# A decoder layer's channel mixer: first product by seven block products for eight, part of the weight sums by accumulating DMA, second product by quarters

## The chip, the cores and the metric

One core of a Trainium2 chip runs the kernel. The metric is device time in microseconds (us) of one execution; the number compared is the median of the runs shown. Engines: PE is TensorE (matmul; PEld is its weight load), DVE is VectorE, ACT is ScalarE, POOL is GpSimd, SP is SyncE, which only issues DMAs here.

## The reference

One inference step of a one-layer decoder: 560 tokens (16 meta, 512 prompt, 32 decode), 1024 channels, 4096 channels in the mixer, all float32. Only the last lines concern the change:

```
h = rms_norm(x, g_mix); proj = h @ w_in            # conv branch and delta-rule branch from proj
...
x = x + mix @ w_o
hm = rms_norm(x, g_mlp) @ w_up                     # first product, 1024 -> 4096
x = x + jnp.square(jax.nn.relu(hm)) @ w_down       # second product, 4096 -> 1024
y = rms_norm(x, g_final)
```

## The kernel before

Channels lie on partitions and tokens on columns. Every large product goes by output tiles of 128 channels by 544 tokens (16 meta tokens are dropped by then), in two halves of 272 tokens (`NPH`). The operands are float32 split in a high and a low part, so each tile of 128 channels of the sum takes three matmuls per half: high weights by high input, high by low, low by high. A tile of a product over 1024 channels is thus 8 x 3 x 2 = 48 matmuls of 128 x 128 weights by 272 columns. They accumulate in a tile `pg` of PSUM with 2 x 512 columns, a half of the tokens in each 512; two such tiles take turns (`psg`, `bufs=2`).

The order of all instructions is written out by a planner at build time (class `Weaver`): streams of work (generators) yield an engine, a modelled cost and what they wait for; the stream whose next instruction could start earliest in the model emits it, and at equal starts the one with the lower priority number. The engines run their queues in that order; semaphores between engines are put in by the framework from the tiles that each instruction reads and writes.

The streams that matter here:

- `weights_dma` (L510) loads one chunk of weights, 128 x 1024, by SP into `wraw`; two chunks are in flight.
- `weights_prep` splits a chunk: ACT writes the high part `wh` (L526), DVE the low part `wl` (L541). For chunks 12 to 61, in earlier stages, ACT writes the negative high part (L535) and POOL adds the chunk to it by an accumulating DMA (L537).
- `gemm` issues the matmuls (L574), and a stream empties each tile of PSUM.
- `ev_wo` (output projection, 8 tiles): DVE adds the tile to the residual `x1` (L1702), ACT and DVE split x1 * g_mlp into `hx` in buffer `R1` (L1706, L1708), ACT squares and DVE sums for the norm (L1715, L1718). `mlp_norm` makes 1 / (mean square + eps) in `r2` (L1728, L1730): it is applied after the second product.
- `ev_up` (first product, 32 tiles): ACT relu from PSUM (L1749), square (L1752), high part (L1754); DVE low part (L1756).
- `ev_dn` (second product): DVE multiplies the tile by `r2` (L1771) and adds it to `x1` (L1774).
- `last_half`: the last tile of the second product goes by halves of the tokens: 48 x 2 matmuls for the first half are followed by those of the second, while DVE empties the first half of the same `pg` tile (L1823), and the final norm of that half begins.

The order of the stages: w_in's products, then w_cout's and w_dout's, then 8 tiles of w_o, 16 tiles of the first product, 8 tiles of the second over the first 2048 channels (two chunks, 96 matmuls each), 16 more of the first, 8 more of the second, and the final norm.

Of the kernel before, what the change touches and what calls it, by code (L numbers as in the profile page):

```python
# [14 lines left out]
P = 128  # L15
# [8 lines left out]
# the first token that the queries need, for their short convolution  # L24
# [8 lines left out]
# columns of the packed per-channel vectors  # L33
# [9 lines left out]
# columns of the packed constants  # L43
# [3 lines left out]
def gemm_order():  # L47
    glu = [[("gb", r), ("ga", r)] for r in range(8)]
    qvz = [[("q", h), ("v", h)] + ([("z", h - 1)] if h else []) for h in range(H)]
    gd = [("gd", c) for c in range(8)]  # L50
    seq = [("k", h) for h in range(8)]
    for x in glu[:6] + qvz[:1] + glu[6:7] + qvz[1:3] + glu[7:] + qvz[3:]:
        seq += x
    seq += gd[:4] + [("z", 7)] + gd[4:]
    for kind in ("do", "gc", "co"):
        seq += [(kind, c) for c in range(8)]
    seq += [("wo", c) for c in range(8)]
    seq += [("up", f) for f in range(16)]
    seq += [("dn0", c) for c in range(8)]
    seq += [("up", f) for f in range(16, 32)]  # L60
    seq += [("dn1", c) for c in range(8)]
    return seq


def n_chunks(kind):
    return 2 if kind in ("dn0", "dn1") else 1


class Tm(float):
    """A modelled time, with the engine that produces it."""  # L70
# [4 lines left out]
class Weaver:  # L75
    """Interleaves in-order streams of instructions by a rough model of the engines."""
# [4 lines left out]
    # how long an engine may wait for a more urgent stream  # L81
# [72 lines left out]
def build(tc, i, o):  # L154
# [15 lines left out]
    with ExitStack() as ctx:  # L170
# [27 lines left out]
        # ---------------------------------------------------------------- constants  # L198
# [13 lines left out]
        # statistics of the delta rule, [token, head, tile]  # L212
# [26 lines left out]
        # ---------------------------------------------------------------- start: x, RMSNorm, h  # L239
# [18 lines left out]
        def warm(n):  # L258
            """Products of ones while the operands come: the tensor engine's clock falls when it rests."""
# [6 lines left out]
        def start():  # L266
# [38 lines left out]
            # sum of squares over channels  # L305
# [52 lines left out]
        def split_x(g, tx, tw):  # L358
            """The parts of x * g_mix, for the first products, whose results take the norm's factor per token."""
# [93 lines left out]
        def mean_bcast(acc, n, rb, ta):  # L453
            """The mean over the channels of acc's sums, on all partitions."""
# [14 lines left out]
        def norm_bcast(acc, rb, t):  # L469
            """1 / sqrt(mean + eps) of acc's sums over the channels, on all partitions."""  # L470
# [26 lines left out]
        # ---------------------------------------------------------------- weights and products  # L497
        seq = gemm_order()
        NW = sum(n_chunks(s[0]) for s in seq)

        def weights_dma():
            yield wait("w_go")
            for n in range(1, NW):
# [7 lines left out]
                E(("raw", n)).set(dma_t(t, 128 * 4096))  # L511

        def weights_prep():
            for n in range(NW):
# [28 lines left out]
                E(("prepl", n)).set(t)  # L543

        rhs_of = {}

        def gemm():
            src_of = {"do": "o", "co": "c", "wo": "m", "up": "x", "dn0": "f0", "dn1": "f1"}
            n = 0
            for idx, (kind, c) in enumerate(seq):  # L550
# [4 lines left out]
                nchk = n_chunks(kind)  # L555
# [3 lines left out]
                steps = [(ch, part, k) for ch in range(nchk) for part in (0, 1) for k in range(8)]  # L559
                # the last product goes by halves of the tokens  # L560
                last = idx == len(seq) - 1
                for h0, h1 in ((0, 1), (1, 2)) if last else ((0, 2),):
                    for ch, part, k in steps:
                        m, row = n + ch, 8 * ch + k
                        if part:
                            tp = yield wait(("prepl", m))
                        else:
                            tp = yield wait(("preph", m) if m else ("preph", 0, k // 4))
                        tk = yield wait((src, row))
                        hi, lo = rhs_of[src](row)  # L570
                        for w, x in ((wls, hi),) if part else ((whs, hi), (whs, lo)):
                            t = yield op("pe", (h1 - h0) * (N / 2400 + 0.0027), tp, tk, tf)
                            for hf in range(h0, h1):
                                nc.tensor.matmul(pt[:, hf, 0:N], w[m][:, k, :], x[:, off + hf * N:off + hf * N + N],  # L574
                                                 start=row == 0 and not part and x is hi,
                                                 stop=row == 8 * nchk - 1 and part == 1)
                        if k == 7:
                            E(("mm" if part else "mmh", m)).set(t)
                    if last:
                        W.spawn(last_half(h0, pt, t), -3 * h0)  # L580
                n += nchk
                if last:
                    W.spawn(warm(NTAIL), -4)
                else:
                    W.spawn(evac(idx, kind, c, pt, t), -3)

        def evac(idx, kind, c, pt, t):
            t = yield from {"k": ev_k, "q": ev_q, "v": ev_v, "z": ev_z, "gb": ev_gb, "ga": ev_ga,
                            "gd": ev_gate, "gc": ev_gate, "do": ev_do, "co": ev_co, "wo": ev_wo, "up": ev_up,
                            "dn0": ev_dn, "dn1": ev_dn}[kind](idx, kind, c, pt, t)  # L590
# [7 lines left out]
        # ---------------------------------------------------------------- beta, g and the decays  # L598
        def g_stage(bk, t):
# [21 lines left out]
            # log(1 + e) = ln(w) + (e - (w - 1)) / w with w = fl(1 + e)  # L621
# [17 lines left out]
            # cumulative sums  # L639
# [28 lines left out]
            # decay matrices of the short segments, all heads: D4[j, h, i]  # L668
# [42 lines left out]
        def d_stage():  # L711
            """Decay matrices D[j, i] = exp(sum of g over (j, i]), zero for i < j."""
# [96 lines left out]
        # ---------------------------------------------------------------- gram matrices of k with their decays  # L809
# [31 lines left out]
        def column_sums(b, sq, sel, t, tb, start=True, stop=True):  # L841
            """Column sums of sq [128, 560] into the rows that sel picks, a quadrant of b for each 128 columns."""
# [23 lines left out]
        def k_norm(hh):  # L866
            """Squared norms of k: columns hh, hh + 8, ... of one bank."""
# [23 lines left out]
        def k_scale(t):  # L891
# [10 lines left out]
            # s = beta / (|k|^2 + 1e-6)  # L902
# [52 lines left out]
        # ---------------------------------------------------------------- (I + K)^-1: blocks of 32 by substitution  # L955
# [105 lines left out]
        # the short segments (decode, prompt tail): blocks of 16 in one lane a head  # L1061
# [922 lines left out]
```

## Time and profile before

| | us |
|---|---|
| median of 3 runs | 1128.67 |
| lowest, highest | 1128.37, 1131.11 |
| span of the profiled execution | 1127.7 |
| output projection, 8 tiles | 677 to 725.5 |
| first product, tiles 0 to 15 | 725.5 to 822.9 |
| second product, first half | 822.9 to 919.4 |
| first product, tiles 16 to 31 | 919.4 to 1016 |
| second product, second half, to its last matmul | 1016 to 1115 |

The span of the profiled execution runs from its first to its last instruction; it is 1.0 us under the median. Idle time of an engine is put down to what ended it.

### The profile page before, as it was taken

The page shows a single profiled execution, that of the slowest core. Times are in us where ns is not written, and L with a number is a line of the kernel's source. Part 1 is how long each engine was busy: PE and PEld are TensorE (multiplying, and loading weights), DVE is VectorE, ACT ScalarE, POOL GpSimd, SP SyncE. Part 2 cuts the span into 40 slices and gives each one's busy share as a digit, 9 for nine tenths or more (in the row PEclk, how much of TensorE's full clock was granted, in tenths as well). Part 3 has the DMA queues.
Part 4 walks back from the last instruction along what each step waited for, and adds up shares of the span by engine and source line. Part 5 has one row for each costly group of instructions (what it writes and reads, how often), then busy time and mean ns, then how long its engine had stood idle before and what let it go on. Part 6 is the DMA issues. An engine that isn't in the chain of part 4 may idle for free.

```text
span 1127.7 us, 21551 instructions
## 1 busy us (share of the span) xinstructions
PE 1097.2 (97%) x8985; PEld 1053.7 (93%) x8985; DVE 663.3 (59%) x1086; ACT 577.1 (51%) x1154; POOL 123.1 (11%) x139
## 2 busy tenths in 40 slices
PE   8999989999989999999899999999999999999996
PEld 6998987999879899999799999999999999999996
DVE  5976996788768877888664355543333233333334
ACT  5586235778768778764247233345421125442320
POOL 2371310102211122221000000000000000000000
PEclk9999998999999999999899999999999999999998
DMA  5223563565556656467624332222332322232222
GB/s 203 76 71 102 123 146 79 126 174 126 143 143 156 149 128 154 135 171 177 151 76 148 100 94 77 92 94 76 94 94 76 94 94 77 93 95 76 94 76 80
DMA packets 49517, 127.71 MB, mean 113 GB/s; under 512 B 13684, under 2 KB 19212, under 8 KB 49420
## 3 DMA queue, kind: packets, MB, share of 16 engines
q1 hardware_dynamic: 42220, 100.12, 28.3%
q0 software_dynamic: 7200, 26.22, 12.5%
q8 instruction: 70, 1.15, 0.4%
q14 instruction: 27, 0.22, 0.1%
HBM read 91.10 MB, written 9.01 MB: 89 GB/s over the span
## 4 chain that ended last, share of the span: by engine, by line
PE 82%; DVE 9%; DMA 5%; issue 2%; ACT 1%; SPq 0%; POOLq 0%; POOL 0%; DVEq 0%; ACTq 0%
PE pg L574 72%; DMA wl<-wraw 2%; DMA wraw<-in_w_dram 2%; DMA M<-in_sd_dram 1%; DMA out_osd_dram<-M 1%; DVE V L1148 1%; DVE M L993 1%; DVE M L990 1%; DVE M L984 1%; DVE RT L997 1%; DVE M L940 1%; PE bk L846 1%; PE bk L1450 1%; PE bk L1370 1%; DVE M L1002 1%
## 5 line engine op out<-in xcount | busy, mean ns | idle before, releaser
L574 PE MATMUL pg<-R,wh 128*128 128x272 f32 (+2 forms) x2944 | 421.0, 294 | 1.6 <-DVE R L427 0.9
L574 PEld LDWEIGHTS pg<-R,wh 128*128 128x128 f32 x2944 | 386.6, 189 | 9.0 <-issue 4.1
L526 ACT ACTIVATE wh<-wraw 128x1024 fp32r<-128x1024 f32 (+1 forms) x153 | 161.3, 1054 | 313.3 <-PE pg L574 239.9
L541 DVE TENSOR_TENSOR wl<-wraw,wh 128x1024 fp32r<-128x1024 f32 x102 | 125.4, 1229 | 175.5 <-PE pg L574 132.7
L574 PE MATMUL pg<-R,wl 128*128 128x272 f32 (+2 forms) x1472 | 218.3, 295 | 0.0
L574 PEld LDWEIGHTS pg<-R,wl 128*128 128x128 f32 x1472 | 197.7, 191 | 3.6 <-issue 2.0
L1148 DVE SCALAR_TENSOR_TENSOR V<-V,vec,V 128x512 f32<-128x512 f32 x240 | 176.1, 767 | 2.9 <-ACT V L1140 0.5
L574 PE MATMUL pg<-RD,wh 128*128 128x272 f32 x512 | 107.9, 291 | 0.5 <-DVE V L1823 0.5
L574 PE MATMUL pg<-K,wh 128*128 128x272 f32 x512 | 108.0, 291 | 0.2 <-DVE K L1678 0.2
L574 PE MATMUL pg<-M,wh 128*128 128x272 f32 x768 | 101.1, 288 | 0.0
L574 PEld LDWEIGHTS pg<-M,wh 128*128 128x128 f32 x768 | 98.2, 188 | 0.0
L574 PEld LDWEIGHTS pg<-RD,wh 128*128 128x128 f32 x512 | 82.1, 191 | 0.8 <-DVE V L1823 0.8
L574 PEld LDWEIGHTS pg<-K,wh 128*128 128x128 f32 x512 | 81.8, 191 | 0.5 <-DVE K L1678 0.5
L537 POOL DMA_DIRECT2D wl<-wraw x50 | 43.7, 874 | 341.7 <-ACT wl L535 199.2
L574 PE MATMUL pg<-RD,wl 128*128 128x272 f32 x512 | 71.7, 292 | 2.2 <-DMA wl<-wraw 2.1
L574 PEld LDWEIGHTS pg<-RD,wl 128*128 128x128 f32 x512 | 67.4, 191 | 2.9 <-DMA wl<-wraw 2.9
L1837 POOL TENSOR_TENSOR ncol<-ncol,misc 68x4 f32<-68x4 f32 x2 | 2.0, 1004 | 536.8 <-DVE ncol L1835 536.8
L535 ACT ACTIVATE wl<-wraw 128x1024 fp32r<-128x1024 f32 x50 | 52.8, 1056 | 4.5 <-PE pg L574 4.5
L1771 DVE TENSOR_TENSOR V<-pg,pre 128x544 f32<-128x544 f32 x15 | 10.9, 725 | 71.4 <-PE pg L574 71.4
L574 PE MATMUL pg<-M,wl 128*128 128x272 f32 x384 | 52.3, 288 | 0.0
L574 PEld LDWEIGHTS pg<-M,wl 128*128 128x128 f32 x384 | 49.9, 188 | 0.0
L783 DVE SCALAR_TENSOR_TENSOR of<-pre,vec,of 128x584 f32<-128x584 f32 x33 | 30.3, 917 | 18.0 <-ACT of L780 17.5
(368 smaller groups left out, 1271.7 us busy)
## 6 DMA issues: line engine op xcount, KB each, us to landing
wraw<-in_w_dram SPq DMA_DIRECT2D x151, 512.0 KB, 3.6
wl<-wraw POOLq DMA_DIRECT2D x50, 512.0 KB, 4.7
M<-in_sd_dram SPq DMA_DIRECT2D x8, 512.0 KB, 4.9
out_osd_dram<-M SPq DMA_DIRECT2D x8, 512.0 KB, 2.8
M<-in_xT_dram SPq DMA_DIRECT2D x8, 280.0 KB, 5.7
V<-in_xT_dram SPq DMA_DIRECT2D x8, 272.0 KB, 5.0
out_oy_dram<-R SPq DMA_DIRECT2D x6, 272.0 KB, 2.3
Ex<-in_sc_dram SPq DMA_DIRECT2D x8, 136.0 KB, 3.8
```

Source lines behind the costliest of these rows:

```text
L526: nc.scalar.activation(wh[:, c[0]:c[1]], w[:, c[0]:c[1]], AF.Copy)
L535: nc.scalar.activation(wl, w, AF.Copy, scale=-1.0)
L537: nc.gpsimd.dma_start(wl, w.bitcast(F32R), accum_op=ALU.add)
L541: nc.vector.tensor_tensor(wl, w, wh.bitcast(F32), op=ALU.subtract)
L574: nc.tensor.matmul(pt[:, hf, 0:N], w[m][:, k, :], x[:, off + hf * N:off + hf * N + N], start=row == 0 and not part and x is hi, stop=row = ...
L783: nc.vector.scalar_tensor_tensor(acc[:, 0:584], pr[:, q:q + 584], vcol(w + q), acc[:, 0:584], op0=ALU.mult, op1=ALU.add)
L846: nc.tensor.matmul(b[32 * j:32 * j + 32, 0:w], sel, sq[:, 128 * j:128 * j + w], start=start, stop=stop)
L940: nc.vector.scalar_tensor_tensor(M1["KT"][:, n, :], b[:, 128 * j:128 * j + 128], st["s"][:, hh, j:j + 1], Ds[hh][:, j, :], op0=ALU.mult, o ...
L984: nc.vector.transpose(L[s].rearrange("p a b -> p a b"), KT[s, :, 32 * q:32 * q + 32].rearrange("p n c -> p c n"))
L990: nc.vector.tensor_tensor(tv, L[:, j + 1:, j:j + 1].to_broadcast([P, n, j + 1]), Tl[:, j:j + 1, 0:j + 1].to_broadcast([P, n, j + 1]), op=A ...
L993: nc.vector.tensor_tensor(Tl[:, j + 1:, 0:j + 1], Tl[:, j + 1:, 0:j + 1], tv, op=ALU.subtract)
L1148: nc.vector.scalar_tensor_tensor(cc[:, 0:512], G[r][:, 16 + q:528 + q], vcol(w + q), cc[:, 0:512], op0=ALU.mult, op1=ALU.add)
```

## The change

The first product goes by groups of two output tiles (`g`, 16 groups). In a group the weights are a 2 x 2 matrix of blocks (output tile by even or odd channel tiles of the input; 4 x 128 channels by 128) and the input another (even or odd channel tiles by halves of the tokens). The 2 x 2 block product is made of seven block products instead of eight, each 4 x 3 = 12 matmuls of 272 columns, by sums of blocks on both sides and of the results:

- Input sums T1 to T4 are made once, by DVE, while the output projection runs (`mix_in`, in place of L1706 and L1708), and split in high and low parts by ACT and DVE.
- Weight sums: `P3` and `P1` come from a load and an accumulating DMA that POOL issues from DRAM onto it (`mlp_sums`); `P2` and `P4` are two more adds on DVE. The seven blocks of a group are split by half-chunks of 512 columns (ACT high, DVE low) into a ring of six.
- The results lie in four accumulators: W and Y are the halves of one `pg` tile, X and Z those of the other. Product 1 goes to X; ACT copies X (`s1`); product 6 is added onto X; ACT copies X (`u2`); product 7 is added; ACT copies X negated (`u3`). W takes product 2, Y product 4, Z product 5. DVE forms the four blocks of the result: C11 from W and `s1`, C21 from Y and `u3`, C22 from Z and `u3`; then product 3 is added onto Z, and DVE forms C12 from Z and `u2`. ACT's relu, square and high part and DVE's low part follow as before, for two tiles a group.
- The order of a group is 1, then 3 of the group before, then 2, 6, 4, 7, 5; in the last group of a set 1, 3 of the group before, 2, 6, 5, 7, 4, 3.
- The second product goes by quarters of its 4096 channels (48 matmuls a tile, 32 tiles in all, each emptied by L1771 and L1774), and the stages are now five groups, quarter 0, four groups, quarter 1, four groups, quarter 2, three groups, quarter 3.
- Buffers are placed anew; comments are taken out. The products up to w_o are unchanged.

The diff, cut to its core:

```
+MLP = [("up", (0, 1, 2, 3, 4)), ("dn", 0), ("up", (5, 6, 7, 8)), ("dn", 1), ("up", (9, 10, 11, 12)), ("dn", 2),
+       ("up", (13, 14, 15)), ("dn", 3)]
+PROD = {1: ("A11", "B11", "X"), 2: ("A12", "B21", "W"), 3: ("P4", "B22", "Z"), 4: ("A22", "T4", "Y"),
+        5: ("P1", "T1", "Z"), 6: ("P2", "T2", "X"), 7: ("P3", "T3", "X")}
+def up_order(groups):
+    out, prev = [], None
+    for g in groups:
+        last = g == groups[-1]
+        out.append((g, 1))
+        if prev is not None:
+            out.append((prev, 3))
+        out += [(g, m) for m in ((2, 6, 5, 7, 4, 3) if last else (2, 6, 4, 7, 5))]
+        prev = g
+    return out
...
+        def mix_in(c, t):
+            t = yield op("act", act_c(NPOST) + 0.07, t)
+            nc.scalar.activation(b[:], x1[c][:], AF.Copy, scale=vcol(V_GMLP + c))
+            t1 = yield op("act", act_c(n), t)
+            nc.scalar.activation(hi, bb, AF.Copy)
...
+            t1 = yield op("dve", dve_c(n), t1)
+            nc.vector.tensor_tensor(lo, bb, hi.bitcast(F32), op=ALU.subtract)
+            if not odd:
+                return
...
+            nc.vector.scalar_tensor_tensor(tb[:, one], ta[:, one], -1.0, b[:, two], op0=ALU.mult, op1=ALU.subtract)
+            nc.vector.tensor_tensor(tb[:, two], tb[:, one], b[:, one], op=ALU.add)
+            nc.vector.tensor_tensor(ta[:, two], b[:, two], b1[:, two], op=ALU.subtract)
+            for q, x, tx in ((6, tb, t), (4, ta, t3)):
+                nc.scalar.activation(a[q], x[:], AF.Copy)
+                nc.vector.tensor_tensor(a[q + 1], x[:], a[q].bitcast(F32), op=ALU.subtract)
...
+        def mlp_sums(g, rb, t):
+            t = yield op("pool", 1.0, t)
+            nc.gpsimd.dma_start(rb, i["wu"][g][:, 1024:2048], accum_op=ALU.add)
...
+                    if nm == "P2":
+                        nc.vector.tensor_tensor(rc[:, 0:512], rb[:, 512:1024], ra[:, 512:1024], op=ALU.add)
+                        nc.vector.tensor_tensor(rc[:, 512:1024], rc[:, 0:512], ra[:, 0:512], op=ALU.add)
...
+                if s >= 6:
+                    tf = yield wait(("bmm", s - 6))
+                nc.scalar.activation(hi, raw, AF.Copy)
+                nc.vector.tensor_tensor(lo, raw, hi.bitcast(F32), op=ALU.subtract)
...
+        def up_gemm(groups):
+            n0, wy, tf0 = yield from pg_tile()
+            n1, xz, tf1 = yield from pg_tile()
+            acc = {"W": (wy, 0), "Y": (wy, 1), "X": (xz, 0), "Z": (xz, 1)}
+            for g, m in up_order(groups):
+                wn, bn, an = PROD[m]
+                pt, hf = acc[an]
+                if m in (6, 7):
+                    tf = yield wait(("upc", g, {6: "s1", 7: "u2"}[m]))
+                elif m == 3:
+                    tf = yield wait(("upc", g, "C22"))
+                elif g != groups[0]:
+                    tf = yield wait(("upc", g - 1, {1: "u3", 2: "C11", 4: "C21", 5: "C12"}[m]))
+                for part in (0, 1):
+                    for kp in range(4):
...
+                        for w, x in ((wl, hi),) if part else ((wh, hi), (wh, lo)):
+                            t = yield op("pe", NPH / 2400 + 0.0027, tp, tk, tf)
+                            nc.tensor.matmul(pt[:, hf, 0:NPH], w[:, kp, :], x,
+                                             start=kp == 0 and not part and x is hi and m not in (3, 6, 7),
+                                             stop=kp == 3 and part == 1, skip_group_check=True)
...
+        def up_copies(g, acc):
+            x = acc["X"][0][:, acc["X"][1], 0:NPH]
+            for k, (nm, m, sc) in enumerate((("s1", 1, 1.0), ("u2", 6, 1.0), ("u3", 7, -1.0))):
+                nc.scalar.activation(up["k"][k][:], x, AF.Copy, scale=sc)
+        def up_c(g, acc, an, nm, m, k, need, dst):
+            a = acc[an][0][:, acc[an][1], 0:NPH]
+            in0, in1, o_ = (up["k"][k][:], a, ALU.subtract) if nm == "C22" else (a, up["k"][k][:], ALU.add)
+            nc.vector.tensor_tensor(dst, in0, in1, op=o_)
...
+        def dn_gemm(q):
+            for c in range(8):
+                n, pt, tf = yield from pg_tile()
+                steps = [(p_, k) for ks in ((0, 1, 2, 3, 4, 5), (6, 7)) for p_ in (0, 1) for k in ks]
```

## Rows read from the trace of the kernel before

**Rows 1.** The page: busy time, share of the span and instructions of each engine; then the chain that ended last, its shares of the span by engine.
```profile
PE 1097.2 (97%) x8985; PEld 1053.7 (93%) x8985; DVE 663.3 (59%) x1086; ACT 577.1 (51%) x1154; POOL 123.1 (11%) x139
PE 82%; DVE 9%; DMA 5%; issue 2%; ACT 1%; SPq 0%; POOLq 0%; POOL 0%; DVEq 0%; ACTq 0%
```
**Rows 2.** Busy time by stretch: length, then PE, PEld, DVE, ACT and POOL busy in us (instructions), granted clock, busy share of the DMA engines, GB/s. An earlier stretch with accumulating DMAs, then the four mixer stages.
```profile
200.00:300.00 100.00, 99.84 (x813) 92.95 (x811) 81.26 (x155) 77.57 (x205) 15.87 (x23) 1.00 0.59 144
...
725.50:822.90 97.40, 97.40 (x773) 96.92 (x772) 36.20 (x36) 48.12 (x65) 0.00 (x0) 1.00 0.28 87
822.90:919.40 96.50, 96.50 (x770) 96.50 (x769) 29.20 (x31) 18.92 (x19) 0.00 (x0) 1.00 0.29 88
919.40:1016.00 96.60, 96.60 (x772) 96.60 (x771) 31.75 (x33) 46.14 (x61) 0.00 (x0) 1.00 0.28 88
1016.00:1100.00 84.00, 84.00 (x671) 84.00 (x670) 29.10 (x32) 25.26 (x29) 0.00 (x0) 1.00 0.26 82
```
**Rows 3.** Timeline of PE in the first product, one tile and the start of the next: start, length, engine, line, operation, number.
```profile
738.68 4.18 PE L574 MATMUL pg<-R,wh 128*128 128x272 f32 x32
742.70 2.17 PE L574 MATMUL pg<-R,wl 128*128 128x272 f32 x16
744.71 4.18 PE L574 MATMUL pg<-R,wh 128*128 128x272 f32 x32
```
**Rows 4.** Timeline of PE, PEld and DVE where the last tile of the second product goes from the first half of the tokens to the second; in brackets the idle time before and what ended it.
```profile
1106.90 0.29 PE L574 MATMUL pg<-RD,wh 128*128 128x272 f32 x1
...
1107.02 0.28 PE L574 MATMUL pg<-K,wh 128*128 128x272 f32 x1
1107.34 0.44 DVE L1823 TENSOR_TENSOR V<-pg,pre 128x272 f32<-128x272 f32 x1 [2.81 <-PE pg L574]
...
1107.84 0.19 PEld L574 LDWEIGHTS pg<-RD,wh 128*128 128x128 f32 x1 [0.75 <-DVE V L1823]
1107.84 0.39 PE L574 MATMUL pg<-RD,wh 128*128 128x272 f32 x1 [0.53 <-DVE V L1823]
...
1108.07 0.29 PE L574 MATMUL pg<-K,wh 128*128 128x272 f32 x1
```
**Rows 5.** Groups of instructions by line from 740 us to the end: number, busy us, mean ns of one, idle before.
```profile
L541 DVE TENSOR_TENSOR wl<-wraw,wh 128x1024 fp32r<-128x1024 f32 x61 | 74.6, 1223 | 147.4 <-PE pg L574 113.5 <-ACT wh L526 23.1 <-issue 10.8
L526 ACT ACTIVATE wh<-wraw 128x1024 fp32r<-128x1024 f32 x60 | 63.7, 1061 | 176.9 <-PE pg L574 176.6
L1749 ACT ACTIVATE zs<-pg 128x544 f32<-128x544 f32 x30 | 18.8, 626 | 28.4 <-PE pg L574 28.4
L1771 DVE TENSOR_TENSOR V<-pg,pre 128x544 f32<-128x544 f32 x15 | 10.9, 725 | 71.4 <-PE pg L574 71.4
L1752 ACT ACTIVATE of<-zs 128x544 f32<-128x544 f32 x15 | 9.9, 659 | 0.5
L1756 DVE TENSOR_TENSOR K<-acc,RD 128x544 fp32r<-128x544 f32 x8 | 5.8, 726 | 6.1 <-ACT RD L1754 6.1
L1827 ACT ACTIVATE zs<-V 128x272 f32<-128x272 f32 x2 | 0.9, 432 | 11.5 <-DVE V L1825 11.5
```
**Rows 6.** DMA issues: number, KB each, median us from issue to landing.
```profile
wraw<-in_w_dram SPq DMA_DIRECT2D x151, 512.0 KB, 3.6
wl<-wraw POOLq DMA_DIRECT2D x50, 512.0 KB, 4.7
```
**Rows 7.** Timeline of all engines where the output projection ends and the first product begins.
```profile
725.53 4.19 PE L574 MATMUL pg<-R,wh 128*128 128x272 f32 x32
725.73 0.73 DVE L1702 TENSOR_TENSOR V<-pg,V 128x544 f32<-128x544 f32 x1 [2.86 <-PE pg L574]
...
726.49 0.76 ACT L1706 ACTIVATE R<-V,vec 128x544 fp32r<-128x544 f32 x1 [1.67 <-DVE V L1702]
727.15 0.64 ACT L1715 ACTIVATE zs<-V 128x544 f32<-128x544 f32 x1
```
**Rows 8.** Timeline of the end on DVE: the last half of the last tile is emptied, and the last eight outputs.
```profile
1115.35 0.44 DVE L1823 TENSOR_TENSOR V<-pg,pre 128x272 f32<-128x272 f32 x1
...
1121.07 2.52 DVE L1851 TENSOR_TENSOR R<-V,bk 128x272 f32<-128x272 f32 x7 [3.15 <-PE bk L1841]
```
**Rows 9.** Timeline of PE after a wait of 2.12 us, in an earlier stage.
```profile
537.95 3.40 PE L574 MATMUL pg<-RD,wl 128*128 128x272 f32 x16 [2.12 <-DMA wl<-wraw]
541.15 0.66 PE L574 MATMUL pg<-RD,wh 128*128 128x272 f32 x2
...
542.05 0.44 PE L574 MATMUL pg<-RD,wh 128*128 128x272 f32 x2
542.34 0.42 PE L574 MATMUL pg<-K,wh 128*128 128x272 f32 x2
```
**Rows 10.** Timeline of PE at a wait of 1.53 us, in the stage of the heads.
```profile
394.04 0.65 PE L1474 MATMUL bk<-M,kq 128*32 128x128 f32 x16 [1.53 <-DMA M<-in_sd_dram]
```
**Rows 11.** Busy time of stretches around these two waits, columns as in Rows 2; the granted clock is the third number from the end.
```profile
540.00:543.00 3.00, 3.00 (x18) 3.00 (x18) 1.58 (x3) 0.06 (x1) 0.00 (x0) 0.65 0.88 225
543.00:546.00 3.00, 3.00 (x27) 3.00 (x26) 2.86 (x5) 2.09 (x3) 0.75 (x1) 1.00 0.36 143
...
365.00:400.00 35.00, 33.47 (x272) 29.94 (x271) 26.70 (x59) 26.50 (x81) 6.20 (x6) 1.00 0.52 127
400.00:450.00 50.00, 50.00 (x404) 46.04 (x404) 39.74 (x80) 42.48 (x126) 13.88 (x12) 1.00 0.62 151
```

More of the change, by code (lines that the diff above doesn't have):

```diff
@@ L498, in build @@
         seq = gemm_order()
-        NW = sum(n_chunks(s[0]) for s in seq)
+        NW = len(seq)
         def weights_dma():
@@ L558, in gemm @@
                 off = Q0 if kind == "q" else META if kind in ("z", "gd", "gc") else 0
[L559 to L564, printed above, removed]
+                for part in (0, 1):
+                    for k in range(8):
                         if part:
-                            tp = yield wait(("prepl", m))
+                            tp = yield wait(("prepl", idx))
@@ L567, in gemm @@
                         else:
-                            tp = yield wait(("preph", m) if m else ("preph", 0, k // 4))
-                        tk = yield wait((src, row))
-                        hi, lo = rhs_of[src](row)
+                            tp = yield wait(("preph", idx) if idx else ("preph", 0, k // 4))
+                        tk = yield wait((src, k))
+                        hi, lo = rhs_of[src](k)
                         for w, x in ((wls, hi),) if part else ((whs, hi), (whs, lo)):
[L572 to L585, printed above, removed]
+                            t = yield op("pe", 2 * (N / 2400 + 0.0027), tp, tk, tf)
+                            for hf in range(2):
+                                nc.tensor.matmul(pt[:, hf, 0:N], w[idx][:, k, :], x[:, off + hf * N:off + hf * N + N],
+                                                 start=k == 0 and not part and x is hi, stop=k == 7 and part == 1)
@@ new lines, in build, with up_tiles @@
+        up = {}
+        def up_tiles(g):
+            if g == 0:
+                yield wait(("wosq", 7))
+            if g == 1:
+                yield wait(("mixin", 3))
+            if g in (5, 9, 13):
+                for c in (6, 7):
+                    yield wait(("dn", (g - 5) // 4, "add", c))
+            if g >= 2:
+                for f in (2 * g - 4, 2 * g - 3):
+                    yield wait(("upr", f))
+            up[g] = [T(x, [P, NPOST]) for x in (("zs0", "zs1") if g % 2 == 0 else ("V8", "V9"))]
+            E(("uptile", g)).set(0.0)
@@ new lines, in up_out1, with up_out2 @@
+        def up_out1(g, acc):
+            yield wait(("uptile", g))
+            c = up[g][0]
+            yield from up_c(g, acc, "W", "C11", 2, 0, "s1", c[:, one_])
+            t = yield from up_c(g, acc, "Z", "C12", 3, 1, "u2", c[:, two_])
+            yield from up_act(2 * g, c, t)
+        def up_out2(g, acc):
+            yield wait(("uptile", g))
+            c = up[g][1]
+            for nm in (("C21", "C22") if g in four_first else ("C22", "C21")):
+                an, m = ("Y", 4) if nm == "C21" else ("Z", 5)
+                t = yield from up_c(g, acc, an, nm, m, 2, "u3", c[:, one_ if nm == "C21" else two_])
+            E(("upc", g, "C22+")).set(t)
+            yield from up_act(2 * g + 1, c, t)
@@ L1744, in ev_up, with f_tile, up_act @@
+        four_first = [g for kind, a in MLP if kind == "up" for g in a[:-1]]
+        def f_tile(f):
+            j = f % 10
+            if ("f", j) not in fhl:
+                fhl[("f", j)] = (T(f"RD{j}", [P, NPOST], F32R)[:], T(f"K{j}", [P, NPOST], F32R)[:]) if j < 8 else ring["f"][j - 8]
+            fhl[f] = fhl[("f", j)]
+            return fhl[f]
+        def up_act(f, c, t):
+            if f >= 10:
+                yield wait(("dnq", (f - 10) // 8))
             if f >= 2:
-                yield wait(("f%d" % ((f - 2) // 16), (f - 2) % 16))
@@ L1763, in ev_dn @@
+        def ev_dn(idx, q, c, pt, t):
             tr = yield wait("r2")
-            E(("dn0m", c)).set(t)
             if c >= 2:
-                yield wait((kind, "add", c - 2))
-            elif kind == "dn1":
-                yield wait(("dn0", "add", 6 + c))
+                yield wait(("dn", q, "add", c - 2))
+            elif q:
+                yield wait(("dn", q - 1, "add", 6 + c))
+            if c < 2:
+                for f in range(8 * q + 4, 8 * q + 8):
+                    yield wait(("upr", f))
```

313 lines of the change are left out of this document (263 added, 50 removed).

## The prediction

> **What bounds the kernel now.** I read the page's busy shares first: PE is busy in 97% of the span, and the chain that ended last lies on it for 82% [rows 1]. The busy time by stretch says where: in all four mixer stages PE is busy in the whole stretch at a granted clock of 1.00 (the upper level, 2.4 GHz), while DVE and ACT stand at 19 to 50% and the DMA engines at 26 to 29% [rows 2]. The timeline gives the rate. One tile of the first product starts at 738.68, the next at 744.71: 48 matmuls in 6.03 us, 125.6 ns each [rows 3]. Inside the mixer nothing but the number of matmuls, or a new wait on PE, can move the end.
>
> **What the change removes.** First product before: 32 tiles x 48 = 1536 matmuls. After: 16 groups x 7 products x 12 = 1344 of the same shape. 192 fewer x 0.1256 = **24.1 us gained**. The second product keeps its count (16 x 96 = 32 x 48).
>
> **What it adds on PE: waits on a PSUM tile.** X and Z are two halves of one tile, W and Y of the other. Before, a mixer tile is filled whole and then emptied whole, so only one place shows what happens when PE fills one half while another engine reads the other: the last tile. There two matmuls of the second half go through, then PE waits until DVE's read of the first half (L1823) has ended, though its own data have long been there [rows 4]. That DVE started only after those two matmuls says the same from the other side. So in this program readers and writers of a two-half tile are kept in order as for one object. The price: the second matmul starts at 1107.02, the fourth at 1108.07, 1.05 us instead of two pitches (0.25): **0.80 us a wait**, with a DVE read of 0.44 us [rows 4].
>
> The Trainium skill speaks against such a wait: in "PSUM — Partial Sum Buffer", sections "PSUM bank collisions raise a hardware error" and "Summary: rules for kernel authors", accesses to different banks run clean and a reader beside running matmuls should target a different bank. A bank is 2 KiB by that page, so the halves are different banks and the chip needs no wait; the row shows that this program waits nevertheless. By the rule the forecast would be the first rival's time, below.
>
> Now the same place in the new order 1(X), 3 of the group before (Z), 2(W), 6(X), 4(Y), 7(X), 5(Z), next 1(X):
> - `s1` reads X after product 1; PE goes on with product 3 in Z: a wait.
> - `u3` reads X after 7; PE goes on with 5 in Z: a wait.
> - C22 reads Z after 5; PE goes on with the next group's 1 in X: a wait.
> - `u2`, C12, C11 and C21 are followed by a product in the other tile, 1.51 us (12 x 0.1256) that cover a read of 0.4 us: nothing.
>
> The first group of a set has no product 3 behind its 1 (no `s1` wait); the last goes 6, 5, 7, 4, 3 and has waits at `s1` and `u2` alone. Per set of n groups that is 3(n - 1) + 1: sets of 5, 4, 4, 3 make 13 + 10 + 10 + 7 = **40 waits**. Most can't be escaped: were the planner to put the `u3` or C22 read (or the last group's `u2`) later than the next product, the product behind that one needs its value. Only the 12 `s1` waits could go, which leaves 28.
>
> Length: an ACT copy of 272 columns from PSUM has no row. 272 from SBUF took 432 ns (L1827); from PSUM 544 took 626 (L1749) against 659 from SBUF (L1752) [rows 5], so some 0.40 and a wait of 0.76. From below 0.76; from above 0.80 plus half of an ACT instruction that happens to run (0.66 / 2), 1.13. I take 0.80: the planner gives these reads the lowest priority number, and ACT and DVE have room (below). **40 x 0.80 = 32.0 us lost**, between 28 x 0.76 = 21.3 and 40 x 1.13 = 45.2. Behind each such wait stand all of PE's later matmuls; for PE wait the next combines, relu and the splits of weights whose ring slot it frees.
>
> **Stage changes.** A set takes both tiles at once, and product 1 goes into X, in the tile that the stage before filled last. So PE waits until that tile is emptied, where before the other tile was free. Three times it is L1771 with 0.725 [rows 5]: 0.80 + 0.725 - 0.44 = 1.08 each, 3.3 us; up to 5.4 if an add of 0.72 stands ahead on DVE. Once it is L1702 with 0.73 [rows 7]: 1.1. There the input of the last channel tile is late too: before, L1706 ran right behind L1702 [rows 7]. Now, counted from the last w_o matmul: L1702 ends at 1.04; on ACT two half-chunks of weights (half of 1.06 each [rows 5]) and the square (0.64) stand ahead of the scaling copy (0.76 [rows 7]), then the high part 0.66, then DVE's low part 0.73 behind two sums of 0.44: ready at some 4.5. PE reaches that operand, the last quarter of product 2, at 1.2 + 1.5 + 0.75 = 3.5. I take 0.9 (0 if nothing stands ahead, 2.5 if every sum does). Stage changes together **5.3 us**, from 4.3 to 9.
>
> **The end.** The last tile's second half now lasts 24 matmuls (3.0 us) instead of 48, so the two final passes of DVE meet. The second begins its last outputs 5.7 us after L1823 [rows 8], when the first's eight (some 3 us) are nearly done: **0.5 us**, 0 to 1.
>
> **What I cost at nothing, and its cover.** ACT in a group: 7 half-chunks x 0.53 + 3 copies x 0.43 + 6 passes of 544 x 0.66 = 9.0 us; DVE: 9 x 0.61 + 4 x 0.44 + 2 x 0.73 = 8.7 [rows 5]. A group takes PE 84 x 0.1256 = 10.55 us, with three waits 12.95. Both fit, at 70% and 67%, where they now have 30 to 50%; without that cover each read waits for the one in front, which is the upper price above. SP's queue gets three loads a group instead of two and POOL one accumulating DMA: 1.79 MB in 12.95 us, 138 GB/s, while the stretch from 200 to 300 moved 144 with the same kind of DMA and PE at 99.8% [rows 2]. An accumulating DMA landed 4.7 us after issue, a load 3.6 [rows 6]; from DRAM it has no row: between 4.7 and twice that. Load, issue and sum make 3.6 + 0.9 + 9.4 = 14 us at most, and the buffer is free about 18 us before the sum is first read, since weights are split six products ahead and two buffers take turns. The `rb` load that waits for its buffer holds `rd` and the next `ra` behind it on SP; these too have over a group of lead. The twice as frequent L1771 and L1774 are 1.45 us of DVE per 6.03 us tile, beside PE.
>
> **Sum.** Span 1127.7 - 24.1 + 32.0 + 5.3 + 0.5 = 1141.4; the median lies 1.0 above the span: **1142.4 us**, 1.2% slower. A group's pair of tiles takes 12.95 us where it took 12.06.
>
> **The rivals.**
> - *PE isn't made to wait for the other half.* Then 1128.7 - 24.1 + 5.3 + 0.5 = **1110.4**. For it: `hx` in R1 was written for the last channel tile (L1706 to 727.25) while PE read other parts of R1 without a wait from 725.53 on [rows 7], so the order is not kept by whole buffers everywhere. Against: the only row on a PSUM tile's halves [rows 4]. It decides for faster where a wait costs under (24.1 - 5.8) / 40 = 0.46 us, hardly more than the read itself. Chance 0.08.
> - *Few and short waits.* 28 x 0.76 and stage changes of 4.3: 1128.7 - 24.1 + 21.3 + 4.3 = **1130**, no change within what can be told. It needs every `s1` to be issued over a product late. Chance 0.07.
> - *The clock falls too.* After a wait of 2.12 us PE ran 22 matmuls from 537.95 to 542.34, 4.39 us instead of 2.76, at a granted clock of 0.65 in 540 to 543 (part of it at the lower level, 1.2 GHz) [rows 9, 11]: 1.6 us lost. A wait of 1.53 us left the clock at 1.00 [rows 10, 11]. The waits at C22 and `s1` lie one product apart, 1.1 to 1.4 us of rest together. If each of the 12 such pairs brought a fall: 12 x 1.6 = 19, **1162**; half of them, 1152. Against: a single wait is 0.53 to 0.75 us of rest [rows 4], and PE works in over 80% of a group. The Trainium skill has this case in "TensorE: Matmul & The Clock Gate", section "A second HAM failure mode: psum-queue depth-cycling": short rests between groups of matmuls can make the clock swing. No row here shows it for rests this short. Chance 0.11.
>
> **Chances and range.** Forecast 0.74 (its own range 1132 to 1155, from the bounds of its terms), rivals 0.08, 0.07 and 0.11. The range, 1131 to 1157, leaves out the first rival, part of the second and the upper half of the third. A measurement of this kernel can tell 0.3% (3.4 us) from no change: faster 0.08, same 0.06, slower 0.86.
>
> **What would show it.** Right: in the first product, groups of about 13 us; PE idle 0.5 to 0.8 us before some 40 matmuls of `up_gemm`, ended by ACT's copies of X (about two thirds) and DVE's C22; the idle lies a few matmuls inside products 3, 5 and 1, not at their start; 1344 + 1536 mixer matmuls at 125.6 ns between waits; PE idle about 1 us at each start of a set. Wrong: groups of 10.6 us with PE full (first rival), a granted clock under 1 in the first product (third), or waits of PE for `bh`, `bl` or a DMA, which I put at nothing: then weights are late and the loss is elsewhere.

## The result, and the profile after

| | us |
|---|---|
| forecast | 1142.4 (1131 to 1157) |
| kernel after, median of 4 runs | 1142.68 (1141.68 to 1143.44) |
| kernel before, median of 4 runs beside them | 1128.52 (1128.32 to 1131.11) |
| ratio after to before, 95% interval | 1.0123 (1.0107 to 1.0140) |
| span of the profiled execution after | 1141.6 |

Slower by 1.2%, as forecast. The page first: PE has fewer matmuls and less busy time than in [rows 1], and a smaller share of a longer span; of the chain that ended last ACT has gone from 1% to 3% and DVE from 9% to 11%, the DMAs stayed at 5%.

```profile
PE 1083.6 (95%) x8793; PEld 1029.5 (90%) x8793; DVE 776.3 (68%) x1350; ACT 630.3 (55%) x1330; POOL 138.2 (12%) x155
PE 79%; DVE 11%; DMA 5%; ACT 3%; issue 2%; SPq 0%; POOL 0%; POOLq 0%; DVEq 0%; ACTq 0%
```

Busy time by stretch, columns as in [rows 2], from the first set of the first product to the last matmul of the second: a set, a quarter, and so on in turns.

```profile
727.55:797.78 70.23, 59.24 (x426) 55.26 (x425) 49.41 (x82) 42.91 (x82) 2.59 (x3) 0.98 0.40 98
797.78:846.02 48.24, 48.24 (x387) 48.24 (x385) 23.55 (x36) 13.42 (x23) 1.73 (x2) 1.00 0.52 142
846.02:895.76 49.74, 44.68 (x338) 42.50 (x337) 32.59 (x56) 30.73 (x59) 1.72 (x2) 1.00 0.38 97
895.76:943.99 48.23, 48.23 (x386) 48.23 (x385) 23.55 (x36) 13.41 (x23) 1.75 (x2) 1.00 0.54 142
943.99:993.75 49.76, 44.70 (x339) 42.53 (x337) 32.58 (x56) 30.74 (x59) 1.74 (x2) 1.00 0.40 97
993.75:1041.87 48.12, 48.12 (x386) 48.12 (x385) 23.55 (x36) 13.40 (x23) 1.72 (x2) 1.00 0.50 139
1041.87:1078.82 36.95, 33.40 (x255) 31.87 (x253) 23.88 (x41) 22.20 (x43) 0.86 (x1) 1.00 0.30 84
```

The quarters are full, 48.24 of 48.24 us. The sets are not: in the second, third and fourth PE rests about a tenth of the time, at a granted clock of 1.00 and with DVE and ACT idle for a third of it. What ended PE's idle time from 720 us on (us in total, times, the longest):

```profile
PE pg L1980 <- ACT KT L2023: 6.1, 12, 0.5
PE pg L1980 <- ACT Ex L2023: 5.8, 12, 0.5
PE pg L1980 <- DVE V L2032: 3.7, 7, 0.5
PE pg L1980 <- DVE zs L2032: 2.6, 5, 0.5
PE pg L1980 <- DVE pre L1793: 2.5, 1, 2.5
PE pg L1980 <- ACT Tt L2023: 1.9, 4, 0.5
```

L1980 is the matmul of `up_gemm`, L2023 the copies of X, L2032 the combines. KT is `s1` (12 waits), Ex is `u3` (12), Tt is `u2` (4, the last group of each set), V and zs are the blocks C22 (12): the 40 waits, place by place. One wait in the timeline of PE, after product 7 in X:

```profile
742.68 0.66 PE L1980 MATMUL pg<-R,whm 128*128 128x272 f32 x4
743.83 0.65 PE L1980 MATMUL pg<-M,whm 128*128 128x272 f32 x3 [0.49 <-ACT Ex L2023]
```

Four matmuls of product 5 go into Z; then PE stands until ACT's copy of the other half has ended. It is the picture of [rows 4] with ACT in DVE's place.

**Where the time went.** The mixer, from its first matmul to the end, took 1127.7 - 725.5 = 402.2 us and takes 1141.6 - 727.55 = 414.1. By terms (42.00 us, a set of four groups without the waits, is measured in the first experiment):

| term | forecast | measured, and from what |
|---|---|---|
| 192 matmuls fewer | -24.1 | -25.2: 1344 at 42.00 / 336 = 168.0, against twice the 96.60 of [rows 2] |
| 40 waits | +32.0 | +31.0: (49.74 - 42.00) + (49.76 - 42.04) + (36.95 - 31.51) = 20.9 over 27 waits, 0.774 each |
| start of the first set | +2.0 | +6.9: 70.23 - 420 x 0.125 - 13 x 0.774 = 7.7, less 0.8 before (97.40 - 96.60) |
| three changes from a quarter to a set | +3.3 | 0: the quarters' 144.6 against 1.5 x 96.5 |
| end | +0.5 | -0.7: 1141.6 - 1078.82 = 62.8, against 111.7 - 48.25 |
| sum over the mixer | +13.7 | +12.0 |

The span is 13.9 longer. The other 2.0 us lie ahead of the mixer, whose first matmul starts at 727.55 instead of 725.53 [rows 7]; the experiments below, with the same products ahead of it, start theirs anywhere from 719.9 to 744.7, so I don't put them down to the change. Some executions in the experiments run longer, at a granted clock of 0.95 or 0.96 ahead of the mixer instead of 0.98 or 0.99; the ratios leave out those over 1.5% above the fastest of their kernel, the medians count them, and the traces of e2, e4, e5 and e7 are of such executions.

### The profile page after: what moved, and what is told of

The parts are those of the page before. It is cut to its first block, busy times and chain, and to the rows that moved or that the text cites. A ratio compares the mean times of both kernels' runs of the same rounds, so it can differ in the third digit from the quotient of the medians.

```text
span 1141.6 us, 21769 instructions
## 1 busy us (share of the span) xinstructions
PE 1083.6 (95%) x8793; PEld 1029.5 (90%) x8793; DVE 776.3 (68%) x1350; ACT 630.3 (55%) x1330; POOL 138.2 (12%) x155
## 4 chain that ended last, share of the span: by engine, by line
PE 79%; DVE 11%; DMA 5%; ACT 3%; issue 2%; SPq 0%; POOL 0%; POOLq 0%; DVEq 0%; ACTq 0%
PE pg L595 36%; PE pg L2101 17%; PE pg L1980 15%; DMA wl<-wraw 2%; DMA wraw<-in_w_dram 1%; DVE V L1162 1%; DVE M L1007 1%; DVE M L1004 1%; DVE acc L797 1%; PE bk L860 1%; DVE of L797 1%; DVE M L998 1%; DVE RT L1011 1%; DVE M L954 1%; PE bk L1464 1%
## 5 line engine op out<-in xcount | busy, mean ns | idle before, releaser
L595 PE MATMUL pg<-R,wh 128*128 128x280 f32 (+2 forms) x1920 | 286.8, 296 | 1.6 <-DVE R L452 0.9
L595 PEld LDWEIGHTS pg<-R,wh 128*128 128x128 f32 x1920 | 255.7, 189 | 9.0 <-issue 4.1
L552 ACT ACTIVATE wh<-wraw 128x1024 fp32r<-128x1024 f32 (+1 forms) x89 | 93.4, 1049 | 126.4 <-PE pg L595 62.8
L595 PE MATMUL pg<-R,wl 128*128 128x280 f32 (+2 forms) x960 | 147.7, 298 | 0.0
L595 PEld LDWEIGHTS pg<-R,wl 128*128 128x128 f32 x960 | 130.3, 191 | 3.8 <-issue 2.1
L1884 POOL DMA_DIRECT2D RT<-in_wu_dram x16 | 13.9, 869 | 452.4 <-DVE wl L567 129.9
L1980 PE MATMUL pg<-R,whm 128*128 128x272 f32 x340 | 60.7, 292 | 6.7 <-ACT KT L2023 4.0
L567 DVE TENSOR_TENSOR wl<-wraw,wh 128x1024 fp32r<-128x1024 f32 x38 | 47.2, 1242 | 28.5 <-PE pg L595 19.2
L1980 PEld LDWEIGHTS pg<-R,whm 128*128 128x128 f32 x340 | 49.0, 188 | 9.5 <-ACT KT L2023 5.8
L2101 PE MATMUL pg<-K,whm 128*128 128x272 f32 x272 | 56.3, 288 | 0.0
L2101 PE MATMUL pg<-RD,whm 128*128 128x272 f32 x272 | 56.2, 288 | 0.0
L595 PE MATMUL pg<-K,wh 128*128 128x272 f32 x256 | 53.6, 291 | 0.2 <-DVE K L1692 0.2
L1980 PE MATMUL pg<-R,M 128*128 128x272 f32 x258 | 47.5, 294 | 3.7 <-ACT KT L2023 2.1
```

Of the source, the lines that this page charges most:

```text
L552: nc.scalar.activation(wh[:, c[0]:c[1]], w[:, c[0]:c[1]], AF.Copy)
L567: nc.vector.tensor_tensor(wl, w, wh.bitcast(F32), op=ALU.subtract)
L595: nc.tensor.matmul(pt[:, hf, 0:N], w[idx][:, k, :], x[:, off + hf * N:off + hf * N + N], start=k == 0 and not part and x is hi, stop=k == ...
L1980: nc.tensor.matmul(pt[:, hf, 0:NPH], w[:, kp, :], x, start=kp == 0 and not part and x is hi and m not in (3, 6, 7), stop=kp == 3 and part ...
L2101: nc.tensor.matmul(pt[:, hf, 0:NPH], w[:, k % 4, :], x[:, hf * NPH:hf * NPH + NPH], start=n_ == 0 and x is hi, stop=n_ == len(steps) - 1)
```

## The experiments

Theory: the wait for the half of a two-half PSUM tile that another engine reads is the loss (31 us), and it comes with the tile, not with the bank. Rivals: the seven-product order makes PE wait for something else (late weight splits, the combines themselves, the accumulating DMA), which would keep the sets long whatever tile Z lies in.

So that the stages ahead of the mixer don't blur the comparison, each row gives, beside the median and the ratio to the kernel before on that chip, the mixer's own length in the trace: the span less the start of its first matmul. It is 402.2 before and 414.1 after. Each is the length in one execution.

| run | median us | ratio to before, 95% interval | mixer us |
|---|---|---|---|
| e1_z_own_tile | 1119.54 | 0.9821 (0.9739 to 0.9904) | 384.5 |
| e2_pair_xy_wz | 1143.0 | 1.0107 (1.0008 to 1.0206) | 406.0 |
| e3_norm_late | 1139.36 | 1.0084 (1.0052 to 1.0116) | 412.3 |
| e4_sums_by_dve | 1142.3 | 1.0114 (1.0052 to 1.0176) | 415.7 |
| e5_z_own_tile_again | 1112.04 | 0.9872 (0.9845 to 0.9899) | 383.4 |
| e6_z_own_norm_late | 1109.27 | 0.9842 (0.9814 to 0.9870) | 381.6 |
| e7_z_own_sums_dve | 1124.56 | 0.9911 (0.9879 to 0.9943) | 386.3 |
| e8_z_own_norm_late_inputs_first | 1107.25 | 0.9835 (0.9813 to 0.9857) | 379.7 |

**Z in a tile of its own (e1, and e5 for a cleaner time).** Z goes into a tile of one bank (512 columns); before it had the second 512 columns of X's tile. Products, order and readers stay.

```
-            acc = {"W": (wy, 0), "Y": (wy, 1), "X": (xz, 0), "Z": (xz, 1)}
+            zb, kz, tz = yield from get_bank()
+            acc = {"W": wy[:, 0, 0:NPH], "Y": wy[:, 1, 0:NPH], "X": xz[:, 0, 0:NPH], "Z": zb[:, 0:NPH]}
...
```

> The changed kernel with one edit: accumulator Z lies in a PSUM tile of its own (a small bank that is free in these stages), so X and Z no longer share one. Theory (PE waits because X and Z are two halves of one tile): all 40 waits of 0.5 us rest go, 40 x 0.757 = 30 us; groups of 10.6 us; 1142.7 - 30.3 = 1112. Rival 1 (the waits are the time in which a value is handed from PE to ACT or DVE and back, which the order of products doesn't cover): they stay, only in other places, 1138 to 1143. Rival 2 (ACT and DVE, at 9 us or more a group, can't keep up with 10.6 us): groups of 11 to 12 us and waits of PE for split weights or combines, 1118 to 1130.

> The same kernel as in e1_z_own_tile (accumulator Z in a PSUM tile of its own), for a clean time. Theory (the 40 waits are the whole of the loss against the saved matmuls, bar the start of the first set): mixer stages 384.7 us again, so some 17.6 us under the kernel before: 1111 us, a ratio of 0.984 to 0.987. Rival (part of what was measured was that chip's noise in the earlier stages): the mixer's length in the trace differs from 384.7 by more than 1 us, or the ratio is nearer 1 than 0.99.

Busy time of e1's second to fourth set, and what PE still waits for at its products in the mixer:

```profile
829.71:871.71 42.00, 42.00 (x339) 42.00 (x338) 32.14 (x56) 30.14 (x59) 1.72 (x2) 1.00 0.44 115
...
919.95:961.99 42.04, 42.04 (x339) 42.04 (x338) 32.13 (x56) 30.12 (x59) 1.73 (x2) 1.00 0.43 114
...
1010.11:1041.62 31.51, 31.51 (x255) 31.51 (x253) 23.52 (x41) 21.77 (x43) 0.86 (x1) 1.00 0.36 93
```

```profile
PE pg L1981 <- DVE pre L1793: 4.0, 1, 4.0
```

All 40 waits are gone, PE is full in these sets, and a group takes 42.00 / 4 = 10.5 us. DVE and ACT do the same work in less time and are not in the way; no weight, sum or DMA is late. That settles the cause. In time, e5 is a mixer of 383.4 us in the trace, 18.8 under before, and by its ratio 1.28% under before, 14.4 us by 0.0128 x 1128: some 4 us less than the mixer's part, and at the edge of what I expected (0.987). Those lie ahead of the mixer, where this chip's executions differ by more than that; I leave them open. The mixer is also 1.3 us from the 384.7 that I gave, where I had named 1 us as the rival's sign. The two traces of this one kernel are 1.1 us apart, all of it in the first set (61.55 us in e1, 60.34 in e5), where PE waited 4.0 and 2.7 us for L1793. So differences of a microsecond between two traces say nothing there.

**X paired with Y, W with Z (e2).** One line; the tiles' release follows their last reader.

```
-            acc = {"W": (wy, 0), "Y": (wy, 1), "X": (xz, 0), "Z": (xz, 1)}
+            acc = {"W": (wy, 0), "Z": (wy, 1), "X": (xz, 0), "Y": (xz, 1)}
```

> The changed kernel with the accumulators paired otherwise: X with Y in one tile, W with Z in the other. Theory (shared tile): a read stalls PE where the next product goes to the other half of the same tile: now u2 (X, then product 4 in Y) and C12 (Z after product 3, then product 2 in W), only in groups that are not the last of a set: 2(n - 1) a set, 24 in all instead of 40; 16 x 0.757 = 12 us less, 1130.6. Rival 1 (handing over of values, whatever the tile): no change, 1142 to 1143. The waits' releasers must change from s1, u3 and C22 to u2 and C12.

What PE waits for in e2, and the busy time of its second set:

```profile
PE pg L1980 <- ACT Tt L2022: 5.8, 12, 0.5
PE pg L1980 <- DVE V L2031: 3.7, 7, 0.5
PE pg L1980 <- DVE zs L2031: 2.7, 5, 0.5
...
PE pg L1980 <- ACT Ex L2022: 1.9, 4, 0.5
```

```profile
856.72:904.43 47.71, 44.16 (x339) 42.47 (x338) 32.48 (x56) 30.65 (x59) 1.73 (x2) 1.00 0.39 102
```

28 waits, not the 24 I had counted: in the last group of a set product 4 goes into Y right behind `u3`'s read of X. The waits have moved to the readers whose next product now shares their tile (`u2` and C12), and `s1`, C22 and most `u3` have lost theirs. The mixer is 8.1 us shorter for 12 waits fewer, 0.67 each; the second set, with three waits fewer, 2.03. The median doesn't show it: it is 1143.0, where I had 1130.6 and the rival 1142 to 1143, from executions between 1135.85 and 1156.53, and the ratio's interval (1.0008 to 1.0206) has room for both. What decides here is the waits, place by place, and the sets. Each accumulator has 512 columns to itself in all three versions; whether PE waits for its reader goes by what shares the tile.

**The norm later (e3).** The norm of the mixer was to stand less in the way at the start of the first set: in the planner it waits for product 3 of group 4, and the reciprocal is costed with 3.55 us.

```
+            t = yield wait(("upm", 4, 3))
             t = yield from mean_bcast(ml["ss"], NPOST, r2, t)
...
-            t = yield op("dve", dve_c(NPOST), t)
+            t = yield op("dve", 3.55, t)
```

> The changed kernel with the mixer's norm (the sum over channels by PE, and the reciprocal of 3.5 us on DVE) issued after the first set of groups instead of at its start; r2 is needed only by the second product. Theory (the first set loses 6.6 us against the tile rate plus its 13 waits because the norm's matmul stands in PE's queue and its reciprocal stands on DVE ahead of the low part of T2 and T4): 4 us less, 1138.5, and no wait of 2.5 us for that low part. Rival (PE would stand there anyway for the low part of the last channel tiles, made some 3 us after the last w_o matmul): 2 us less or nothing, 1141 to 1143. If the norm comes too late for quarter 0 it shows as PE waiting at its third tile.

```profile
PE pg L1981 <- DVE D L1777: 2.5, 1, 2.5
```

This row of e3's waits of PE stands in the place of the 2.5 us for L1793: the input of the last channel tiles is late by itself. The first set is 3.2 us shorter (67.04 for 70.23), the first quarter 1.0 longer, the mixer 1.8 shorter in this one trace, and the ratio's interval (1.0052 to 1.0116) meets that of the kernel after. The rival was nearer than my theory.

**The sums by DVE (e4 with the two-half tile, e7 with Z apart).** The accumulating DMAs go; DVE makes `P3` and `P1` with two more adds of 512 columns a group.

```
-                    W.spawn(mlp_sums(x, rb, dma_t(t, 128 * 4096)), 0)
+                    E(("rb", x)).set(dma_t(t, 128 * 4096))
...
+                        nc.vector.tensor_tensor(rb[:, 0:512], rb[:, 0:512], rb[:, 512:1024], op=ALU.add)
...
+                        nc.vector.tensor_tensor(rb[:, 512:1024], rb[:, 512:1024], rd, op=ALU.add)
```

> The changed kernel without the accumulating DMAs: the sums P3 and P1 are two more adds of 512 columns on DVE for each group, from the same loads. Theory (a group lasts 12.8 us because of its waits, and DVE has 9.4 us of work in it): the 1.4 us hide, 1142.7 within 1.5. Rival (DVE's queue delays the reads that PE waits for): each of the 12 C22 waits, and some u3 waits, grows by half of an add or more, 1147 to 1152.

> Z in its own tile, and the sums P1 and P3 by DVE instead of the accumulating DMA (two adds of 512 columns more a group on DVE). Theory (the accumulating DMA was hidden while PE waited 2.3 us a group, and is worth something once groups take 10.55 us): DVE has 8.7 + 1.4 = 10.1 us a group at the durations of the trace, 96% of a group, so sets 2 and 3 get over 42.04 us by 0.5 to 3 us each, with PE waits ended by DVE's low parts of weights or combines. Rival (DVE still fits): sets 2, 3 and 4 within 0.3 us of 42.0, 42.0 and 31.5, time as in e5.

The second set of e4, then of e7:

```profile
864.11:913.85 49.74, 44.68 (x338) 42.48 (x337) 35.64 (x62) 30.16 (x59) 0.00 (x0) 1.00 0.21 69
```

```profile
856.57:898.57 42.00, 42.00 (x338) 42.00 (x337) 35.37 (x62) 29.64 (x59) 0.00 (x0) 1.00 0.29 82
```

POOL's transfers are gone, DVE is 3.1 and 3.2 us busier, and these sets are as long as with the DMAs. For e4 I expected that (its first and fourth set are 0.9 and 0.3 longer, the mixer 1.6). For e7 I expected the sets to grow, and was wrong: of nine adds more in a set and the quarter beside it only six fall in the set (62 DVE instructions for 56 in e1), they take 3.2 us, 0.54 each and not 0.69, and DVE stands at 35.37 / 42.00 = 84%. So in the second to fourth set the accumulating DMA buys no time, with the waits or without. For the whole kernel that is not settled. e7's profiled mixer is 2.9 us longer than e5's, 3.4 of it in the first set, where the granted clock fell once more (last section); with one trace of each I don't put that down to the sums. But the two executions in e7's ratio took 1115.20 and 1116.45 us, and the six in e5's 1108.40 to 1114.99: a loss of some 4 us is possible, and these runs don't say where.

**Z apart and the norm later (e6), and the input sums ahead of the weight splits as well (e8).** e6 has the edits of e1 and e3; e8 has them too, and this one:

```
-            W.spawn(mix_in(c, t), 0)
+            W.spawn(mix_in(c, t), -3)
```

> Z in its own tile, and the norm of the mixer waits until product 3 of group 4 in the planner, with the reciprocal costed at 3.55 us. Theory (the inputs of the first group are late by themselves, the wait for the norm only stands on top where nothing else does): the 4.0 us that PE waits for the first output's norm goes, the first set is 1 to 4 us shorter (57.5 to 60.5 instead of 61.55), and the first quarter up to 1 us longer; 1108 to 1111 us. Rival (another input or a combine takes its place in full): first set 61 us or more, time as in e5.

> As e6_z_own_norm_late, and the input sums get a higher priority in the planner (minus 3 instead of 0), before the splits of weights. Theory (the start of the first set is late because the low parts of the last channel tiles queue on DVE and ACT behind other work): the first set loses 2 to 4 us less than in e6, down to 3 us over its matmuls; 1106 to 1109 us. Rival (the last residual tile sets it whatever the order, or the splits of weights then come late): first set within 0.7 us of e6, or longer.

In e6 the first set takes 57.26 us, a little under the 57.5 to 60.5 that I gave, the first quarter 49.26, 1.0 longer: a mixer 1.8 us under e5's and 2.9 under e1's. The rival came true in part: another input of the first group is late in its place, though not in full.

```profile
PE pg L1982 <- DVE D L1777: 2.5, 1, 2.5
```

The first set and the first quarter of e8, then what PE waits for at its products:

```profile
721.80:777.54 55.74, 53.55 (x423) 52.70 (x422) 44.32 (x78) 41.22 (x79) 2.59 (x3) 1.00 0.53 131
777.53:826.79 49.26, 49.26 (x390) 48.78 (x389) 27.30 (x38) 13.97 (x25) 1.73 (x2) 1.00 0.51 139
```

```profile
PE pg L1982 <- DVE pre L1793: 0.9, 1, 0.9
PE pg L1982 <- ACT R L1771: 0.6, 1, 0.6
PE pg L1982 <- DVE R L1777: 0.4, 1, 0.4
PE pg L1982 <- ACT kq L1791: 0.4, 1, 0.4
```

2.3 us of waits in four short pieces are left, the first set is 55.74 - 52.5 = 3.2 us over its matmuls instead of 17.7 after, and the clock stays up. The gain over e6 is 1.5 us, less than the 2 to 4 that I gave and more than the rival's 0.7. e8 is the fastest version that I ran: 1107.25 us, 1.65% under the kernel before (interval 1.4 to 1.9%), with the same seven products.

## Why the prediction was right, and where it wasn't

The main steps held. **The count** of 40 waits is exact, by place and by engine. **The price** was 0.80, read from one wait in a stage that the change doesn't touch; it measured 0.774, which fits an ACT copy of 0.40 us, as estimated, in 28 of the 40 waits. **The saved matmuls** gave 25.2 us against 24.1. **What I costed at nothing** cost nothing: in the second to fourth set DVE was busy for 32.6 and ACT for 30.7 of 49.74 us, in e1 they fitted in 42.00, and the accumulating DMAs landed in 6.8 us at the median, between the ends of 4.7 and 9.4:

```profile
RT<-in_wu_dram SPq DMA_DIRECT2D x24, 512.0 KB, 4.7
RT<-in_wu_dram POOLq DMA_DIRECT2D x16, 512.0 KB, 6.8
```

**The first rival** (PE isn't made to wait for the other half) is refuted for this program; e5, in which PE isn't, took 1112.0 on its chip, where I had put the rival at 1110.4. The Trainium skill's rule, in "PSUM — Partial Sum Buffer", "Summary: rules for kernel authors", that a reader beside running matmuls should target a different bank, is thus not enough here: reader and matmuls were in different banks with the waits and without them. **The second** (28 waits) needed `s1` to be issued over a product late; all 12 were there. **The third** (the clock) did not come where I looked: rests of 0.49 to 0.55 us in pairs a product apart left the granted clock at 1.00 in the second to fourth set. So the case of the Trainium skill's "TensorE: Matmul & The Clock Gate", "A second HAM failure mode: psum-queue depth-cycling" is not shown by rests this short. The clock did fall at the start of the first set, behind a rest of 1.91 us (below).

**The step that failed** is "Stage changes", whose sum of 5.3 hides two errors that nearly cancel. The first: "product 1 goes into X, in the tile that the stage before filled last", 1.08 us three times. All engines at the start of the second set:

```profile
845.52 0.66 PE L2101 MATMUL pg<-RD,wlm 128*128 128x272 f32 x4
...
846.02 0.67 PE L1980 MATMUL pg<-R,whm 128*128 128x272 f32 x4
846.22 0.72 DVE L2126 TENSOR_TENSOR V<-pg,pre 128x544 f32<-128x544 f32 x1 [1.24 <-PE pg L2101]
```

Product 1 runs while DVE still empties the last tile of the quarter: X's tile is the other one, and W, whose first product comes 12 or more matmuls later, has the late one. Cost 0. I had taken the slot from the order of allocation and had no row for it.

The second error: at the start of the first set I counted one late operand (0.9 us) and stopped at product 2. All engines there, only the rows that hold PE up:

```profile
727.75 0.72 DVE L1717 TENSOR_TENSOR V<-pg,V 128x544 f32<-128x544 f32 x1 [1.04 <-PE pg L595]
...
728.39 1.28 DVE L1932 TENSOR_TENSOR wlm<-RT,whm 128x512 fp32r<-128x512 f32 x2
...
730.36 1.39 PE L483 MATMUL bk<-sg,ones 128*128 128x512 f32 x2 [1.91 <-DVE sg L1727]
730.58 0.43 DVE L1777 TENSOR_TENSOR D<-acc,um 128x272 fp32r<-128x272 f32 x1
...
731.82 0.57 PE L1980 MATMUL pg<-um,M 128*128 128x272 f32 x1
...
733.21 3.54 DVE L1808 RECIPROCAL pre<-pre 128x544 f32<-128x544 f32 x1
...
738.93 0.39 PE L1980 MATMUL pg<-pre,whm 128*128 128x272 f32 x1 [2.52 <-DVE pre L1793]
```

DVE splits two half-chunks of weights ahead of the norm's sum and the low part that product 1 needs last (L1777). PE has the norm's matmul (L483) in its queue ahead of the rest of product 1 and stands 1.91 us for it. Then the reciprocal holds DVE for 3.54 us, and the low part of an input sum (L1793), queued behind it, a combine and two splits of weights, comes 2.52 us late for product 6. In 730.5 to 734 the granted clock is 0.58, part of it at 1.2 GHz. Measured: 6.9 us against 2.0. The wait that ends last sets this: the matmul at 738.93 is PE's 32nd and starts 11.4 us after the first, where 31 matmuls take 3.9, and the 7.5 between are nearly all of the 7.7 in the table. So the 1.91 us and the low clock, which lie ahead of it, cost nothing of their own here: in e1, where the clock stays up behind the same 1.91 us, the 32nd matmul starts 11.3 us after the first all the same. What costs is DVE's queue. In e6, with the norm out of the way, the 32nd matmul starts 8.5 us after the first, in e8 7.0. A moved step drags what is queued around it; I had followed the input's chain on each engine, but not the norm's, which passes through PE and DVE at the same moment. In the mixer as a whole the norm alone (e3, e6 against e5) is worth 1.8 us, since the first quarter takes 1.0 back, and the order of the inputs another 1.9, by single traces.

The end came out 0.7 shorter and not 0.5 longer. From the last product to the end it is 13.3 us instead of 12.5, as forecast, but eight matmuls of the final norm (L2157) now fill the wait of [rows 4], and eight others (L2196) come behind the last product where they stood ahead of it.

Against the forecast's 13.7 the mixer's terms give 12.0, and the start of the mixer adds 2.0; so the median fell nearer to the forecast (0.3 us) than its terms deserve.

## What to carry to other kernels

Before two accumulators are put in one tile, list for every reader which product PE runs next: if it goes into the same tile, PE waits, whatever bank it is in, and here 40 such waits of 0.77 us ate a saving of 25 us. A tile of its own for one accumulator turned a kernel 1.2% slower into one 1.3% faster, so count the waits per object that the framework orders, not per bank. Where a stage begins, follow every chain through all queues (here the norm's reciprocal ahead of an input's low part on DVE) to the wait that ends last, since the cover that hides them inside a stage isn't there yet.

## What the runs showed of the hardware

- A reciprocal of 128 x 544 on DVE takes 3.54 us, five times an add of that shape (0.72); the planner's model gave both the same cost.
- DVE's instructions overlap at their ends: two of 128 x 512 in a row take 1.28 us, where one alone has a record of 0.69. A sum of mean durations thus overstates what DVE is asked for.
- At the start of the first set rests of the same length brought different granted clocks.

Stretches of the kernel after and of e1 right behind PE's rest of 1.91 us for the norm's sum; then 750 to 764 us of e5 and of e7, where PE rests 2.69 and 2.66 us for L1793:

```profile
730.50:734.00 3.50, 3.50 (x13) 2.81 (x14) 3.44 (x8) 1.12 (x4) 0.00 (x0) 0.58 0.73 225
```

```profile
723.00:727.00 4.00, 4.00 (x29) 3.51 (x28) 3.96 (x8) 2.82 (x7) 0.45 (x1) 1.00 0.66 197
```

```profile
750.00:764.00 14.00, 11.31 (x88) 11.09 (x87) 10.72 (x15) 7.83 (x16) 0.86 (x1) 0.98 0.38 76
```

```profile
750.00:764.00 14.00, 11.34 (x59) 10.92 (x59) 10.38 (x15) 4.55 (x10) 0.00 (x0) 0.68 0.03 13
```

Behind 1.91 us the clock fell in the kernel after and stayed at the upper level in e1. In e5 it is back at the upper level for most of the stretch, in e7 it falls once more, and 59 matmul records stand where 88 did: this is most of the 3.4 us of e7's first set. In e8, where no rest exceeds 0.85 us, it stays at 1.00 in the whole first set. What decides between falling and staying isn't shown.
